# Softmax ahead of the gate's product, and turned weights split late, in a four-layer hybrid decoder

## The chip, the cores and the metric

The kernel runs on one core of one Trainium2 chip. A core has a matrix engine (TensorE; PE in the profile, PEld for its weight loads), a vector engine (VectorE, DVE), a scalar engine (ScalarE, ACT), a general engine (GpSimd, POOL) and an engine that only issues transfers (SyncE, SP). The metric is the device time of one execution in microseconds (us), taken as the median of several runs.

## The reference

Four layers with a model width of 2048 work on 256 tokens. Each layer normalises its input, makes one combined input projection, runs one of three causal mixers and four heads of attention to a memory of 256 tokens, multiplies all head outputs by SiLU of a gate, projects them back and adds them to the residual. Mixers by layer: latent attention (0), sparse attention with a top-k indexer (1), sliding window with sinks (2), latent again (0).

```python
for i in range(DEPTH):
    h = rmsnorm(x, norm_in[i])
    # kind i % 3: (queries, keys, values ..., mq, gate) = split(h @ w_in)
    self_out = mixer(...)                       # softmax(q k^T * scale + bias, masked) v per head
    mem_out = softmax(mq mk^T / 16) mv          # 4 heads of 256; mk, mv = split(mem_n @ w_mem_kv[i])
    y = concat([self_out, mem_out]) * silu(gate)    # gate has 2048 + 1024 columns
    x = x + y @ w_out[i]
return rmsnorm(x, final_norm)
```

All inputs are 32-bit floats.

## The kernel before, in words

A product of 32-bit precision is made of three products of rounded parts: each operand is split into a high part (a copy on ACT to the type fp32r) and a low part (a subtraction on DVE), and high x high, high x low and low x high are added up in PSUM. `split` does that: `copy_act` at L61, `tensor_sub` at L65. Weights come by transfers that SP issues (`stage`, L208 and L212, tile `wr`, five buffers) and are split as they come (`parts_of`: `wh`, `wl`, three buffers each).

Two routines make the projections, 16 steps of 128 rows (12 or 4 in the latent mixer). `rows_by` gives token rows: in each step it makes six products of 512 columns, L235 to L237, for two halves of tokens. `columns_by` gives columns: in each step and for two halves `j` it makes one product of 512 columns (both parts of the activations against `wh`, L254) and one of 256 (the high part against `wl`, L256), in the order L254, L256, L254, L256. Accumulators (tag "acc") have four PSUM banks; `total` (L262, L263) adds the two halves of a `columns_by` accumulator into `z`.

Every layer is worked in six parts, in the order 4, 0, 1, 2, 3, 5: parts 0 to 3 are groups of mixer heads (four heads in the latent mixer, class `Latent`; eight in the two others, class `Grouped`), parts 4 and 5 are two memory heads each (`memory_project`, `memory_attend`). A part makes its queries, keys and values, and its gate columns (`gate`: `columns_by` twice, then `z`, `hz`, a tanh `th`, and `gT`), all in `project`. Then `attend` makes the scores (`sp`, or `msp`), softmax on DVE and ACT (`masked_softmax`: tiles `u` and `e`), and turns the normalised weights.

`turned` brings two heads' softmax weights (or one memory head's) from rows of queries to rows of keys: DVE transposes blocks of 32 x 32 into `T`; POOL issues one transfer to memory (`turn<-T`, L418) and four back (`pL<-turn`, L423); ACT copies the high part `pH` (L61) and DVE makes the low part in place (`pL`, L427). `T`, `pL` and `pH` have two buffers each. The products with the values (L521, L663, L817, into `o` or `mo`) use `pH` and `pL`, and are multiplied by `gT` (`gated` or `paired`, tile `yt`) and split into `y`.

`attend` is a generator: it yields once after the turn, and then the loop over parts runs the output projection `w_out` of the part before (four chunks of 512 columns, each with 4 steps of `rows_by` and an addition to `x`, L899) ahead of this part's products:

```python
next(steps)
if pending is not None:
    w_out(*pending, False)
*_, y = steps
pending = (part, y)
```

The order of instructions on each engine is not the written one: a planner takes the program and its own estimates of times, and lets each engine take the instruction that is written first among those that it holds ready. Within an engine's queue the order is then fixed. Small tiles share buffers by tag: `u`, `e`, `bs` and the gate's `th` share tag "e" (four), `z`, `hz` and others tag "z" (three), `yt`, `hl` and others tag "t512" (three). `tc.keep_in_program_order` pins an instruction behind the one that is written before it on its engine.

## Time and profile before

| | us |
|---|---|
| median of 3 runs (lowest to highest) | 2668.21 (2661.11 to 2670.98) |
| the profiled execution | 2658.11 |
| span of its instructions | 2656.3 |
| PE busy | 2592.4 (98%) |
| PEld busy | 2224.3 (84%) |
| DVE busy | 1953.0 (74%) |
| ACT busy | 1613.6 (61%) |
| POOL busy | 267.8 (10%) |
| mean granted TensorE clock | 0.995 of full |

A busy time is the part of the span in which the engine had an instruction of the program at work. Matmuls overlap each other, and their ends are modelled, so that a busy PE may still wait for a little in between. Idle time is put down to the instruction that ended it. The stages stand in the span in this order: the memory's keys and values to about 395 us, then the four layers to about 970, 1518, 2014 and 2656 us.

### The profile page before, as it was taken

The numbers are of one execution on the slowest core, as the hardware profiler recorded it, in microseconds if no ns is written. First come the engines' busy times: TensorE is split into PE (matmuls) and PEld (weight loads), VectorE is DVE, ScalarE is ACT, GpSimd is POOL, SyncE is SP. The second block draws the span as 40 slices with busy tenths as digits, with TensorE's granted clock in tenths as the row PEclk, the third lists the DMA queues.
The fourth block names the chain that finished last, engine by engine and source line by source line (L and its number), as shares of the span: only waits on it lengthen the run. The fifth ranks groups of instructions, "written<-read, shape, count | busy, mean of one in ns | idle before, by whom it ended". The sixth has DMA issues, their size and how long they took to land. (4 is left out here: it accounts for less than half of the span.)

```text
span 2656.3 us, 42960 instructions
## 1 busy us (share of the span) xinstructions
PE 2592.4 (98%) x14143; PEld 2224.3 (84%) x14143; DVE 1953.0 (74%) x4413; ACT 1613.6 (61%) x3414; POOL 267.8 (10%) x422
## 2 busy tenths in 40 slices
PE   8999999999999999999999999999999999999997
PEld 7788888888888878888878788878788888888885
DVE  7566656677777776887779676877777767787767
ACT  6455556556665566666667465666665655666554
POOL 1000000010000110011221101211111000000011
PEclk9999999999999999999999999999999999999998
DMA  7888887577768765567787756766776667776774
GB/s 266 276 261 272 274 263 207 157 205 185 192 175 234 214 205 168 164 205 214 227 232 217 212 190 187 235 198 202 219 208 179 200 165 195 195 195 176 228 204 134
DMA packets 472563, 553.65 MB, mean 208 GB/s; under 512 B 74484, under 2 KB 357876, under 8 KB 471188
## 3 DMA queue, kind: packets, MB, share of 16 engines
q1 hardware_dynamic: 440004, 446.69, 57.2%
q0 software_dynamic: 31040, 102.33, 13.4%
q8 instruction: 111, 1.82, 0.3%
q10 hardware_dynamic: 1296, 1.90, 0.2%
q14 instruction: 112, 0.92, 0.1%
HBM read 508.77 MB, written 54.62 MB: 212 GB/s over the span
## 5 line engine op out<-in xcount | busy, mean ns | idle before, releaser
L61 ACT ACTIVATE wh<-wr 128x512 fp32r<-128x512 f32 (+2 forms) x1768 | 1068.6, 608 | 758.7 <-PE acc_g L254 184.3
L65 DVE TENSOR_TENSOR wl<-wr,wh 128x512 fp32r<-128x512 f32 (+2 forms) x1768 | 1156.2, 662 | 499.6 <-ACT wh L61 484.8
L254 PE MATMUL acc_g<-xT,wh 128*128 128x512 f32 x1536 | 520.6, 398 | 3.0 <-DVE z L263 2.9
L256 PE MATMUL acc_g<-xT,wl 128*128 128x256 f32 x1536 | 374.5, 282 | 0.0
L256 PEld LDWEIGHTS acc_g<-xT,wl 128*128 128x128 f32 x1536 | 286.7, 189 | 27.1 <-DVE wl L65 1.2
L254 PEld LDWEIGHTS acc_g<-xT,wh 128*128 128x128 f32 x1536 | 266.1, 189 | 42.7 <-DVE z L263 4.5
L236 PE MATMUL acc_wo<-wl,y 128*128 128x512 f32 x752 | 295.2, 393 | 0.0
L237 PE MATMUL acc_wo<-wh,y 128*128 128x512 f32 x752 | 294.0, 393 | 0.0
L235 PE MATMUL acc_wo<-wh,y 128*128 128x512 f32 x752 | 236.7, 396 | 8.1 <-ACT y L61 6.0
L423 POOL DMA_DIRECT2D pL<-turn x256 | 160.3, 633 | 269.2 <-DMA turn<-T 106.0
L418 POOL DMA_DIRECT2D turn<-T x64 | 48.9, 765 | 1334.5 <-DVE mn L443 455.0
L254 PE MATMUL acc_mq<-xT,wh 128*128 128x512 f32 x512 | 172.6, 397 | 1.0 <-ACT wh L61 1.0
L254 PE MATMUL acc_mk<-mT,wh 128*128 128x512 f32 x512 | 171.6, 397 | 0.0
L235 PEld LDWEIGHTS acc_wo<-wh,y 128*128 128x128 f32 x752 | 136.3, 190 | 37.6 <-ACT y L61 8.9
L237 PEld LDWEIGHTS acc_wo<-wh,y 128*128 128x128 f32 x752 | 141.9, 189 | 29.6 <-DVE y L65 1.1
L236 PEld LDWEIGHTS acc_wo<-wl,y 128*128 128x128 f32 x752 | 142.2, 189 | 29.1 <-DVE wl L65 0.7
L254 PE MATMUL acc_qn<-cT,wh 128*128 128x512 f32 x384 | 128.6, 397 | 0.0
L254 PE MATMUL acc_cq<-xT,wh 128*128 128x512 f32 x384 | 127.8, 395 | 0.0
L899 DVE TENSOR_TENSOR x<-x,acc_wo 128x512 f32<-128x512 f32 x184 | 120.9, 678 | 6.8 <-PE acc_wo L237 6.8
L427 DVE TENSOR_TENSOR pL<-pL,pH 128x768 fp32r<-128x768 f32 (+1 forms) x64 | 57.0, 891 | 92.9 <-ACT pH L61 92.8
L256 PE MATMUL acc_mq<-xT,wl 128*128 128x256 f32 x512 | 125.1, 283 | 0.0
L256 PE MATMUL acc_mk<-mT,wl 128*128 128x256 f32 x512 | 123.0, 281 | 0.0
(297 smaller groups left out, 4790.9 us busy)
## 6 DMA issues: line engine op xcount, KB each, us to landing
wr<-in_w_out_dram SPq DMA_DIRECT2D x192, 512.0 KB, 3.6
wr<-in_w_in_a_dram SPq DMA_DIRECT2D x176, 512.0 KB, 3.8
wr<-in_w_mem_kv_dram SPq DMA_DIRECT2D x128, 512.0 KB, 4.8
wr<-in_w_in_b_dram SPq DMA_DIRECT2D x112, 512.0 KB, 4.1
wr<-in_w_in_c_dram SPq DMA_DIRECT2D x104, 512.0 KB, 3.8
wr<-in_w_uq_dram SPq DMA_DIRECT2D x288, 128.0 KB, 3.4
turn<-T POOLq DMA_DIRECT2D x48, 384.0 KB, 3.9
pL<-turn POOLq DMA_DIRECT2D x192, 96.0 KB, 4.4
```

What stands on the lines that cost most here:

```text
L61: nc.scalar.activation(o, i, AF.Copy, scale=scale)
L65: nc.vector.tensor_sub(lo, src, f32(hi))
L235: nc.tensor.matmul(acc[t][:, :n], xh, wh[:, :n], start=first, stop=False)
L236: nc.tensor.matmul(acc[t][:, :n], xh, wl[:, :n], start=False, stop=False)
L237: nc.tensor.matmul(acc[t][:, :n], xl, wh[:, :n], start=False, stop=last)
L254: nc.tensor.matmul(acc[j], wh[:, o:o + P], q[:, :, kt % 4, :], start=first, stop=False)
L256: nc.tensor.matmul(acc[j][:, 0, :], wl[:, o:o + P], q[:, 0, kt % 4, :], start=False, stop=last)
L418: nc.gpsimd.dma_start(d.rearrange("m p w -> p m w"), T.rearrange("p m j n b -> p m (j n b)"))
L423: nc.gpsimd.dma_start(f32(pL)[j * 32:(j + 1) * 32, :].rearrange("p (i r) -> p i r", r=r), bass.AP(tensor=d.tensor, offset=d.offset + j * r ...
L427: nc.vector.tensor_sub(pL, f32(pL), f32(pH))
L899: nc.vector.tensor_add(xs, xs, acc[t])
```

## The change

Three things are changed. First, a part's gate columns are no longer made in `project`; `project` hands out a function, and the loop calls it after softmax and turn of the part. Second, `turned` becomes a class `Turn` in three steps: `add` transposes a head into `T`, `send` issues the five transfers, and `parts` makes `pH` and `pL`. `parts` is called right ahead of the products, and its copy on ACT is pinned behind what is written before it on ACT. The unsplit weights wait in `pL` with three buffers instead of two or, in every second pair of a `Grouped` part, in one of two spare places beside `vz`; `pH` takes its buffers from tag "T", which has three. Three chunks of the output projection of the part before run ahead of the first half of the products, and the fourth between the halves. Third, `columns_by` makes both products of 512 columns first, and then both of 256.

```diff
@@ columns_by
+                    at = [slice(k * S + j * P, k * S + (j + 1) * P) for j in range(2)]
                     for j in range(2):
-                        o = k * S + j * P
-                        nc.tensor.matmul(acc[j], wh[:, o:o + P], q[:, :, kt % 4, :],
-                                         start=first, stop=False)
-                        nc.tensor.matmul(acc[j][:, 0, :], wl[:, o:o + P], q[:, 0, kt % 4, :],
+                        nc.tensor.matmul(acc[j], wh[:, at[j]], q[:, :, kt % 4, :], start=first, stop=False)
+                    for j in range(2):
+                        nc.tensor.matmul(acc[j][:, 0, :], wl[:, at[j]], q[:, 0, kt % 4, :],
                                          start=False, stop=last)
@@ turned
-    def turned(heads, planes):
...
+    class Turn:
+        def __init__(self, n, planes, raw=None):
...
+            self.T = wk.tile([P, 768], F32, name="T", tag="T", bufs=3)[:, :self.size].rearrange(
+                "p (m j n b) -> p m j n b", m=m, j=4, n=n)
+        def add(self, s, es):
...
+                nc.vector.transpose(self.T[:, at[0]:at[-1] + 1:step, :, s, :], ...)
+        def send(self):
...
+            d = dr.tile([m, P, w], F32, name="turn", tag=f"turn{m * w}", bufs=6)
+            nc.gpsimd.dma_start(d.rearrange("m p w -> p m w"), self.T.rearrange("p m j n b -> p m (j n b)"))
+            if self.raw is None:
+                self.raw = wk.tile([P, 768], F32R, name="pL", tag="pL", bufs=3)
+            self.raw = self.raw[:, :self.size]
+            for j in range(4):
+                nc.gpsimd.dma_start(...)
+            return self
+        def parts(self):
+            pH = wk.tile([P, 768], F32R, name="pH", tag="T", bufs=3)[:, :self.size]
+            tc.keep_in_program_order(copy_act(pH, f32(self.raw)))
+            nc.vector.tensor_sub(self.raw, f32(self.raw), f32(pH))
+            return pH, self.raw
@@ memory_project (Latent.project and Grouped.project alike)
-        return nm, kT, v, qT, gate(nm, w, g0 + 2048 + part * 512)
+        return (nm, kT, v, qT), lambda: gate(nm, w, g0 + 2048 + part * 512)
@@ memory_attend (Latent.attend alike)
-            ws.append(turned([es], [(0, 0), (0, 1), (1, 0), (1, 1)]))
-        yield
+            turn.add(0, es)
+            ws.append(turn.send())
+        gT = yield
...
-            pH, pL = ws[h]
+            pH, pL = ws[h].parts()
@@ Grouped.first
+            room = [act.tile([P, 2048], F32R, name="vz", tag=f"big{1 + z}") for z in range(2)]
+            self.vz = [r[:, :1152].rearrange("p (t c) -> p t c", t=2) for r in room]
+            self.raw = [r[:, 1152:1920] for r in room]
@@ Grouped.attend
+                if n_ % 2 == 0:
+                    ws.append(Turn(2, CAUSAL, self.raw[n_ // 4] if n_ % 4 == 2 else None))
+                ws[-1].add(n_ % 2, masked_softmax(score, bias, None, nsk))
+                if n_ % 2 == 1:
+                    ws[-1].send()
+            gT = yield
...
                 for u in range(2):
+                    pp = ws[2 * z + u].parts()
@@ the loop over parts
             next(steps)
+            gT = gating()
             if pending is not None:
-                w_out(*pending, False)
-            *_, y = steps
+                w_out(*pending, False, range(3))
+            y = steps.send(gT)
+            if pending is not None:
+                w_out(*pending, False, range(3, 4))
+            y = next(steps)
             pending = (part, y)
```

## The prediction, made before the changed kernel ran

> **What bounds the kernel now.** I read the page first (busy times, then the idle time before each group), then the list of waits, then the instruction timeline and the chain of waits at the places that the waits name.

> ```profile
> span 2656.3 us, 42960 instructions
> ...
> PE 2592.4 (98%) x14143; PEld 2224.3 (84%) x14143; DVE 1953.0 (74%) x4413; ACT 1613.6 (61%) x3414; POOL 267.8 (10%) x422
> ```

> PE (TensorE) is the bound: it idles for 2656.3 - 2592.4 = 63.9 us. A change can win there, or by making the same matmuls follow each other more closely. The list of waits for PE says what ends its idle time (us in total, times, longest):

> ```profile
> PE o L817 <- ACT pH L61: 9.5, 9, 2.3
> PE mo L521 <- ACT pH L61: 8.8, 7, 2.3
> ...
> PE acc_wo L235 <- ACT y L61: 6.0, 4, 4.4
> ...
> PE acc_g L254 <- DVE z L263: 2.9, 5, 0.6
> ...
> PE o L663 <- ACT pH L61: 2.3, 5, 1.0
> ...
> PE o L817 <- DVE pL L427: 1.4, 3, 0.5
> PE mo L521 <- DVE pL L427: 1.0, 3, 0.3
> ```

> So 9.5 + 8.8 + 2.3 + 1.4 + 1.0 = 23.0 us go to the products of the turned softmax weights (`o`, `mo`), which wait for the high part `pH` or the low part `pL`. Those are late because their transfer is late, and while they wait, ACT and DVE stand still with all that is queued behind (list of waits, whole kernel):

> ```profile
> ACT pH L61 <- DMA pL<-turn: 104.3, 51, 4.7
> DVE pL L427 <- ACT pH L61: 92.8, 54, 4.9
> ```

> One such place, in a sliding-window part, in the timelines of PE and of ACT (start, duration, idle time before in brackets):

> ```profile
> 1791.64 0.28 PE L256 MATMUL acc_g<-xT,wl 128*128 128x256 f32 x1
> 1794.26 0.56 PE L817 MATMUL o<-pH,vz 128*128 128x512 f32 x1 [2.34 <-ACT pH L61]
> ```
> ```profile
> 1789.23 0.78 ACT L61 ACTIVATE e<-e,rc 128x128 f32<-128x128 f32 x2
> 1793.36 0.84 ACT L61 ACTIVATE pH<-pL 128x768 fp32r<-128x768 f32 x1 [3.35 <-DMA pL<-turn]
> ```

> ACT sits in front of `pH` for 3.35 us; the weight splits behind it cannot run, so PE runs dry. The dearest case is the end of the last layer, in the chain of waits:

> ```profile
> 2600.98 0.23 PE acc_wo L237
> ...
> 2603.94 5.68 DMA pL<-turn
> ...
> 2609.64 0.64 ACT pH L61
> ...
> 2611.62 5.40 DMA wr<-in_w_out_dram
> ...
> 2618.19 0.53 ACT y L61
> ...
> 2621.69 0.43 PE acc_wo L235
> ```

> A late `pL` holds `pH`, that holds DVE, DVE's late split frees its `wr` buffer late, the next weight load starts late, and `y` comes 4.4 us late. After that gap a 512-column matmul takes 0.43 us instead of 0.23 for about 13 matmuls (2618.76 to 2624.19): 5.43 - 13 x 0.23 = 2.4 us more.

> **Part 1: softmax, turn and transfer ahead of the gate; the split when the products come.** The same instructions run (64 turned tiles, each one `turn<-T` and four `pL<-turn` transfers, one `pH` copy, one `pL` subtraction); only their place changes. Today a transfer's cover is `w_out` of the part before: 4 chunks x 24 products x 0.23 = 22 us, from which softmax itself is taken. In the new order it is the gate (128 matmuls, 32 groups of four at 0.70 us, see part 3: 22.4 us) and three chunks (16.5 us). The way of the last turned tile in the window above:

> ```profile
> 1790.05 0.63 DVE L415 STREAM_TRANSPOSE T<-e 128x128 f32<-128x128 f32 x2
> ```
> ```profile
> 1791.09 0.75 POOL L418 DMA_DIRECT2D turn<-T  x1 [2.38 <-DVE T L415]
> 1798.99 2.48 POOL L423 DMA_DIRECT2D pL<-turn  x4 [7.15 <-PE acc_g L256]
> ```

> From T to the last issue at 1801.5 is 11.4 us, about 15 with the landing. Eight heads of a sliding part take 46 us (rows below), 6 a head; so a latent (MLA) part's four take some 23 us, a memory part's two 12, and with 15 behind them the cover of 39 us holds. In the grouped parts (sparse and sliding) it is partial. Each wait costs PE more than its idle time: a 512-column matmul is counted busy for 0.40 us, but the next may start after 0.23, so 0.16 us a wait. For `mo` and L663: 8.8 + 1.0 + 2.3 + 15 x 0.16 = 14.5 us; I take 13 of it. For L817: 9.5 + 1.4 + 12 x 0.16 = 12.8 us; I take 7, since the chain from softmax to the last products stays long there. **Term: -20** (bounds 0 and -27.3). The end of the last layer: 4.4 + 0.16 + 2.4 = 7.0 us; what is late next there is the weight load, so I take **-6** (bounds 0 and -7).

> The split's own cost at its new place:

> ```profile
> L61 ACT ACTIVATE pH<-pL x64: 613/844/850, 547.3 to 2620.5; 128x768 fp32r<-128x768 f32 x48, 128x512 fp32r<-128x512 f32 x16
> L427 DVE TENSOR_TENSOR pL<-pL,pH x64: 683/958/961, 548.0 to 2621.9; 128x768 fp32r<-128x768 f32 x48, 128x512 fp32r<-128x512 f32 x16
> ```

> 0.84 + 0.96 = 1.8 us from ACT's start to the low part. It is pinned behind the last weight split of the third chunk. With three `wh` buffers ACT may run up to three steps of 6 x 0.23 = 1.36 us ahead of PE, 4.1 us; that hides it: **0**. Without this cover it is the second rival. On POOL's queue the transfers move ahead of nothing but each other, and the next part's loads stand behind them as before; SP holds weight loads alone. No load is added, and the two spare places for raw weights and a third `pL` buffer (five instead of two) take waits away.

> **What the move costs.** Two windows, the gate alone and `w_out` with softmax beside it (columns: length, then busy of PE, PEld, DVE, ACT, POOL):

> ```profile
> 751.00:773.00 22.00, 22.00 (x127) 19.19 (x126) 13.85 (x25) 11.97 (x22) 0.00 (x0) 1.00 0.60 178
> 774.00:796.00 22.00, 22.00 (x106) 18.46 (x105) 20.51 (x64) 16.25 (x40) 3.22 (x5) 1.00 0.52 146
> ```

> With softmax beside it DVE is at 20.51 of 22 us and PE still loses nothing. `w_out` alone needs DVE for 16 splits and 8 additions; both groups stand on the page (busy us, mean ns):

> ```profile
> L65 DVE TENSOR_TENSOR wl<-wr,wh 128x512 fp32r<-128x512 f32 (+2 forms) x1768 | 1156.2, 662 | 499.6 <-ACT wh L61 484.8
> ...
> L899 DVE TENSOR_TENSOR x<-x,acc_wo 128x512 f32<-128x512 f32 x184 | 120.9, 678 | 6.8 <-PE acc_wo L237 6.8
> ```

> 16 x 0.65 + 8 x 0.66 = 15.7 us (busy time through the count), so softmax is some 5 us of DVE there, and beside the gate DVE comes to 13.85 + 5 = 19 of 22 us, less than it bears today. **0**; without this slack the third rival.

> The second cost is a queue for buffers. The timelines of PE and DVE in that latent part:

> ```profile
> 744.17 0.40 PE L648 MATMUL sp<-kn,qn 128*128 128x256 f32 x2
> ```
> ```profile
> 776.64 0.28 DVE L441 TENSOR_TENSOR u<-sp,caus 128x128 f32<-128x128 f32 x1
> ...
> 777.84 0.42 DVE L383 SCALAR_TENSOR_TENSOR gT<-th,hz 128x256 f32<-128x256 f32 x1
> ```

> The scores lay ready at 745, yet their first use `u` came at 776.64, just as the last gate tile `gT` was made. `u`, `e` and the gate's `th` share four buffers (tag "e"): they are given out in program order. In the new order `th` stands behind all `e` of the part. A sliding part:

> ```profile
> 1743.66 0.28 DVE L441 TENSOR_TENSOR u<-sp,bm 128x128 f32<-128x128 f32 x1
> 1743.87 0.42 DVE L383 SCALAR_TENSOR_TENSOR gT<-th,hz 128x256 f32<-128x256 f32 x1
> ```

> Softmax lasts from 1743.66 to 1790.05, 46 us, twice the gate. So for about 24 us the gate's last accumulator keeps one of the four PSUM banks, and `w_out` works with three. At a chunk's border the second half's bank then waits for the addition (0.68 us, row above). The first half's last product starts 0.45 before the last one, takes 0.40, the addition 0.68: its bank is free 0.63 us after the last product's start, and the next chunk wants it after 0.45. That is 0.2 us if DVE is free, 0.85 if one split is ahead. Eight grouped parts x 3 borders: 5 to 20 us, or 0 if scores fill the gap. I take **+6**, near the lower row since PE's order can take the free half first. The waits for `z` (2.9 us) come from the same shortage; I leave them: **0** (bounds -3.7 and +4).

> **Part 3: the 512-column products first.** In `columns_by` the order becomes L254 L254 L256 L256 instead of L254 L256 L254 L256. The trace already has both, since the planner moved every other step:

> ```profile
> 150.00 0.62 PE L254 MATMUL acc_mk<-mT,wh 128*128 128x512 f32 x2
> ...
> 150.70 0.40 PE L254 MATMUL acc_mk<-mT,wh 128*128 128x512 f32 x1
> ...
> 151.41 0.62 PE L254 MATMUL acc_mk<-mT,wh 128*128 128x512 f32 x2
> ...
> 152.10 0.40 PE L254 MATMUL acc_mk<-mT,wh 128*128 128x512 f32 x1
> ...
> 152.82 0.62 PE L254 MATMUL acc_mk<-mT,wh 128*128 128x512 f32 x2
> ```

> A group that starts with x2 takes 0.70 and 0.69 us (150.00, 151.41), an alternating one 0.71 and 0.72 (150.70, 152.10): 0.02 less, between 0.015 and 0.018 with rounding allowed for. The loops hold 1728 groups (gate 768, mk 256, mq 256, cq 192, qn 192, kn 64), of which half alternate: 864 x 0.018 = 15.6 us. Where PE is held by something else the gain is lost, so I take **-11** (bounds 0 and -15.6).

> [...]

> **Sum:** -20 - 6 - 11 + 6 = -31 us. The profiled execution took 2658.11 us (span 2656.3 and 1.8 around it): 2627. The median of the runs, 2668.21, lies 10.1 above it, so against the median the forecast is 2637 us.

> **Rivals.** [...]
> Second, no change: the wait moves from the transfer to the split. If ACT is not ahead of PE, each of 64 splits keeps PE for 0.4 of its 1.8 us, 26 us: 2637 + 26 = 2663. For it: ACT and DVE are at 75 to 93% in these windows. Against: three weight buffers of lead.
> Third, slower: the queue for "e" buffers. In the grouped parts gate tiles come only after 46 us of softmax, the first products' `yt` waits for them, the next part's `hl` (same buffers as `yt`, tag "t512") waits for `yt`, and softmax of the next part for `hl`. PE's other work in a part is about 74 us (q, gate, `w_out` at 22 each, products and scores 8); if the chain of softmax 46, transfer 15, split and products 5, `hl` and transposes 5 and 9 more for late gate tiles grows to 80, each of 8 parts loses 6 us: 2637 + 48 = 2685. It decides from (31 + 13) / 8 = 5.5 us a part. For it: 46 + 15 already outlasts gate and three chunks. Against: q of the next part (22 us) fills the gap.

> **How the numbers follow.** A difference under 0.5% (13 us) can hardly be told from none here. Chances: my forecast 0.55, first rival 0.20, second 0.13, third 0.12. Faster by over 0.5% (below 2655) is the first two, 0.75; within it 0.13; slower 0.12. The best case takes all bounds: 27.3 + 7 + 15.6 + 3.7 = 53.6, 2615. The range goes from 2610 (the runs spread by some us) to 2664, with the second rival and without the third. The likeliest case's own range is 2615 to 2652.

> **What would show it.** Right: the waits of `o` and `mo` for `pH` under 8 us in total; `pH` waiting for its transfer under 20 us; no gap of 4 us before the last output product; alternating groups gone; PE's idle time about 43 us. Wrong: new waits of acc_wo L235 for `x` L899, or of `o` and `mo` for `pL` in most parts; a longer way from one grouped part's first `u` to the next's; a DVE or ACT busy over 95% beside the gate.

## The result, and the profile after

The changed kernel takes 2594.78 us (median of 4 runs, 2592.04 to 2599.47) against 2667.94 for the kernel before (four runs; the three before the forecast gave 2668.21): ratio 0.9731, 95% interval 0.9707 to 0.9755. It is faster by 73 us, where 31 were forecast; the direction was right, the size was not, and the time lies below the range. The profiled execution took 2595.72 us. Three executions of later groups (one of the kernel before, one each of two variants) were slower by far, at 2795 to 10669 us, and are left out of every median and ratio below. The page of the changed kernel:

```profile
span 2593.9 us, 42976 instructions
...
PE 2559.6 (99%) x14143; PEld 2211.9 (85%) x14143; DVE 1958.3 (75%) x4413; ACT 1602.2 (62%) x3414; POOL 267.8 (10%) x422
```

The same 14143 matmuls run. PE's idle time fell from 63.9 to 34.3 us, and its busy time, which holds matmuls that run slowly or wait a little, by 32.8 us. What ends PE's idle time now (us in total, times, longest; L836, L533 are L817, L521 of before):

```profile
PE o L836 <- ACT pH L61: 6.0, 7, 2.2
PE acc_kvb L235 <- ACT wh L61: 2.9, 2, 2.1
...
PE acc_wo L235 <- ACT y L61: 1.5, 1, 1.5
...
PE mo L533 <- ACT pH L61: 0.3, 1, 0.3
```

The waits for `pH` fell from 20.6 to 6.3 us, and those for `pL` are gone; so is the 4.4 us gap ahead of the last output products (1.5 left) and every wait for `z`. ACT stands in front of `pH` for 34.9 us instead of 104.3 (list of waits, whole kernel; `vz` is here the spare place beside `vz`):

```profile
ACT pH L61 <- DMA vz<-turn: 20.6, 8, 3.9
...
ACT pH L61 <- DMA pL<-turn: 14.3, 8, 3.3
```

The groups of `columns_by` start every 0.70 us, and the alternating ones of 0.71 to 0.72 are gone (timeline of PE, the same place as before):

```profile
149.94 0.63 PE L254 MATMUL acc_mk<-mT,wh 128*128 128x512 f32 x2
...
150.64 0.62 PE L254 MATMUL acc_mk<-mT,wh 128*128 128x512 f32 x2
...
151.34 0.63 PE L254 MATMUL acc_mk<-mT,wh 128*128 128x512 f32 x2
...
152.04 0.62 PE L254 MATMUL acc_mk<-mT,wh 128*128 128x512 f32 x2
```

One thing the forecast saw in a single place only: stretches in which TensorE runs at half its clock. In the kernel before, 1795 to 1798 us, right behind the 2.34 us wait shown in the prediction, PE starts 10 matmuls, and a little later in as long a window, with about the same mix of 512 and 256 columns, 19 (length, busy of PE, PEld, DVE, ACT, POOL, then the granted clock):

```profile
1795.00:1798.00 3.00, 3.00 (x10) 2.61 (x11) 2.00 (x4) 0.77 (x2) 0.00 (x0) 0.51 0.72 259
1799.00:1802.00 3.00, 3.00 (x19) 2.63 (x18) 1.39 (x2) 1.46 (x3) 2.47 (x4) 1.00 0.86 255
```

The profile before has four such stretches while PE works (at 132, 1518, 1795 and 2617 us, 20.5 us in all); the profile after has none. PE counts as busy in them, so they hide in busy time.

To see where the 62.4 us between the two spans went, take every distance from one matmul's start to the next and subtract 0.443 ns for each column of the first (227 ns for 512 columns, near the least steady distance in these traces). What is left over sums to 164.7 us before and 101.5 after; the difference, 63.2, is that of the spans but for 0.8 us:

| over the columns' time, us | before | after | change | forecast |
|---|---|---|---|---|
| waits for `pH` and `pL` at the products | 28.0 | 7.5 | -20.5 | -20 |
| waits for `y` (the last layer's end) | 6.6 | 1.7 | -4.9 | -6, with the clock there |
| under 30 ns a matmul (the order of products) | 56.5 | 47.2 | -9.3 | -11 |
| waits for `z`, and shortage of PSUM banks | 3.7 | 0 | -3.7 | +6 |
| waits for `wh`, `wl` | 16.4 | 9.5 | -6.9 | 0 |
| matmuls at half clock | 8.5 | 0 | -8.5 | in the end's term |
| 100 to 300 ns, too short to show as idle | 21.2 | 11.8 | -9.4 | 0 |
| 30 to 100 ns | 23.8 | 23.8 | 0 | 0 |

### The profile page after: what moved, and what is told of

Read it like the earlier page. It is cut to its first block, busy times and chain, and to the rows that moved or that the text cites. A ratio compares the mean times of both kernels' runs of the same rounds, so it can differ in the third digit from the quotient of the medians.

```text
span 2593.9 us, 42976 instructions
## 1 busy us (share of the span) xinstructions
PE 2559.6 (99%) x14143; PEld 2211.9 (85%) x14143; DVE 1958.3 (75%) x4413; ACT 1602.2 (62%) x3414; POOL 267.8 (10%) x422
## 3 DMA queue, kind: packets, MB, share of 16 engines
q0 software_dynamic: 31040, 102.33, 14.2%
## 4 chain that ended last, share of the span: by engine, by line
PE 91%; DMA 4%; issue 2%; DVE 2%; POOL 1%; ACT 1%; ACTq 0%; POOLq 0%; DVEq 0%
PE acc_g L254 14%; PE acc_g L256 7%; PE acc_wo L236 6%; PE acc_wo L235 6%; PE acc_wo L237 6%; PE acc_mk L254 5%; PE acc_mq L254 4%; PE acc_qn L254 3%; PE acc_cq L254 3%; PE acc_mk L256 2%; PE acc_mq L256 2%; PE acc_mv L236 2%; PE acc_mv L237 2%; PE acc_mv L235 2%; PE acc_qn L256 2%; PE acc_cq L256 2%
## 5 line engine op out<-in xcount | busy, mean ns | idle before, releaser
L61 ACT ACTIVATE wh<-wr 128x512 fp32r<-128x512 f32 (+2 forms) x1768 | 1071.7, 609 | 841.7 <-PE acc_g L254 141.4
L65 DVE TENSOR_TENSOR wl<-wr,wh 128x512 fp32r<-128x512 f32 (+2 forms) x1768 | 1164.9, 663 | 526.4 <-ACT wh L61 495.0
L254 PE MATMUL acc_g<-xT,wh 128*128 128x512 f32 x1536 | 485.7, 396 | 0.0
L256 PEld LDWEIGHTS acc_g<-xT,wl 128*128 128x128 f32 x1536 | 283.8, 188 | 61.8
L256 PE MATMUL acc_g<-xT,wl 128*128 128x256 f32 x1536 | 304.9, 279 | 0.0
L237 PE MATMUL acc_wo<-wh,y 128*128 128x512 f32 x752 | 292.9, 390 | 0.0
L235 PE MATMUL acc_wo<-wh,y 128*128 128x512 f32 x752 | 239.5, 391 | 1.5 <-ACT y L61 1.5
L254 PEld LDWEIGHTS acc_g<-xT,wh 128*128 128x128 f32 x1536 | 235.8, 189 | 0.7
L237 PEld LDWEIGHTS acc_wo<-wh,y 128*128 128x128 f32 x752 | 141.3, 188 | 27.2
L235 PEld LDWEIGHTS acc_wo<-wh,y 128*128 128x128 f32 x752 | 138.5, 188 | 29.4 <-ACT y L61 1.9
L254 PE MATMUL acc_mk<-mT,wh 128*128 128x512 f32 x512 | 160.8, 396 | 2.0 <-ACT wh L61 2.0
L254 PE MATMUL acc_mq<-xT,wh 128*128 128x512 f32 x512 | 162.1, 396 | 0.0
L429 POOL DMA_DIRECT2D pL<-turn x192 | 120.8, 636 | 208.5 <-DMA turn<-T 139.3
L254 PE MATMUL acc_qn<-cT,wh 128*128 128x512 f32 x384 | 121.5, 398 | 0.0
L254 PE MATMUL acc_cq<-xT,wh 128*128 128x512 f32 x384 | 120.8, 396 | 0.0
L918 DVE TENSOR_TENSOR x<-x,acc_wo 128x512 f32<-128x512 f32 x184 | 119.9, 679 | 0.7
L256 PEld LDWEIGHTS acc_mk<-mT,wl 128*128 128x128 f32 x512 | 95.8, 188 | 22.7 <-DVE wl L65 0.4
L256 PEld LDWEIGHTS acc_mq<-xT,wl 128*128 128x128 f32 x512 | 93.5, 188 | 20.5 <-DVE wl L65 1.4
L256 PE MATMUL acc_mq<-xT,wl 128*128 128x256 f32 x512 | 102.7, 280 | 0.6 <-DVE wl L65 0.6
```

The lines of the kernel that those rows point to most:

```text
L61: return nc.scalar.activation(o, i, AF.Copy, scale=scale)
L65: nc.vector.tensor_sub(lo, src, f32(hi))
L235: nc.tensor.matmul(acc[t][:, :n], xh, wh[:, :n], start=first, stop=False)
L237: nc.tensor.matmul(acc[t][:, :n], xl, wh[:, :n], start=False, stop=last)
L254: nc.tensor.matmul(acc[j], wh[:, at[j]], q[:, :, kt % 4, :], start=first, stop=False)
L256: nc.tensor.matmul(acc[j][:, 0, :], wl[:, at[j]], q[:, 0, kt % 4, :], start=False, stop=last)
```

## The experiments

Each kernel was timed beside the kernel before on one chip; ratios are to it. Chips differ between groups (by group, the median of the kernel before lay between 2667.94 and 2677.55 us), so kernels are compared by ratio, or directly within a group.

**One part at a time.** First the order of products alone, put into the kernel before.

```diff
                     for j in range(2):
-                        matmul(acc[j], wh ...); matmul(acc[j][:, 0, :], wl ...)
+                        matmul(acc[j], wh ...)
+                    for j in range(2):
+                        matmul(acc[j][:, 0, :], wl ...)
```

> The kernel before with part 3 alone (both 512-column products of columns_by first). Theory A, the order itself is worth 10 to 18 ns in each of the 864 groups that alternated: 9 to 16 us, so 2652 to 2659 against 2668; PE's idle time stays near 64 us and the waits for pH stay at 20 us or more; the clock stays near 0.995. Rival 1, the order is worth nothing: 2668 within 4. Rival 2, the order carries most of the 73 us (each group also has its low part later, so that waits for wl go): below 2640.

Measured: 2689.57 us, ratio 1.0057 (1.0041 to 1.0072): slower by 15 us, which no theory had. The order did what it should: the row "under 30 ns" fell from 56.5 to 46.9 us. But the waits grew (list of waits for PE; `L817`, `L521` and `L663` are the products with `pH`):

```profile
PE o L817 <- ACT pH L61: 16.3, 12, 4.5
PE acc_wo L235 <- ACT y L61: 12.2, 4, 7.3
PE mo L521 <- ACT pH L61: 12.2, 7, 2.8
PE acc_g L254 <- DVE z L263: 7.7, 5, 1.5
...
PE o L663 <- ACT pH L61: 6.3, 5, 2.6
```

34.8 us for `pH` where it was 20.6, 12.2 for `y` where it was 6.0, 7.7 for `z` where it was 2.9; matmuls at half clock took 22.7 us more than their columns' time instead of 8.5. While a transfer sets when the products may start, a faster PE arrives sooner and waits longer; that alone would take the gain away but make no loss. The longer half-clock time (14.2 us more) can make it one, and so can the planner, which made a new order for the whole program: the instructions on ACT stand in another order at 1457 of 3414 places, those on DVE at 2302 of 4413. The run does not separate the two. In the changed kernel the old order was put back:

```diff
-                    for j in range(2): matmul(acc[j], wh ...)
-                    for j in range(2): matmul(acc[j][:, 0, :], wl ...)
+                    for j in range(2): matmul(acc[j], wh ...); matmul(acc[j][:, 0, :], wl ...)
```

> The changed kernel with the old order of the products (512, 256, 512, 256) put back. Theory A: 9 to 16 us slower than the changed kernel, 2604 to 2611, half of the groups alternating, waits of PE as in the changed kernel. Rival 1: 2595 within 4. Rival 2: above 2625.

Measured: 2611.97 us, ratio 0.9766 (0.9753 to 0.9779), against 0.9731 with the new order (0.9714 when it was timed again, below): 9 to 14 us more. "Under 30 ns" is 56.2 us again, 9.0 above the changed kernel, and waits and clock add a few us. So the new order gains here, and was a loss without the rest.

Then the gate behind softmax, with `w_out` in three chunks and one, but the turn and the early split as before (the order of products kept):

```diff
-            return ..., gate(self.nm, self.w, self.g0 + g * 512)
+            return (...), lambda: gate(self.nm, self.w, self.g0 + g * 512)
...
+            gT = gating()      # after next(steps); turned() unchanged
```

> The order of part 3 and the gate behind softmax, with w_out in 3 + 1 chunks, but the old turn: the split stands right behind the transfers in the program, two buffers each for T, pL and pH. Theory A, half of the gain of the move comes from ACT and DVE no longer standing in front of pH: ACT still idles 50 us or more in front of pH, and the time is 2615 to 2645. Rival, cover is all that counts (the transfers land early, so the place of the split is idle talk): ACT's idle time in front of pH falls below 35 us as in the changed kernel, and the time is 2595 to 2605.

Measured: 2642.46 us, 0.9878 (0.9862 to 0.9894), in theory A's range. And the late split, but the gate at its old place (in the memory parts alike):

```diff
                 at, gating = mixer.project(part)
+                gT = gating()
                 steps = mixer.attend(*at)
             next(steps)
-            gT = gating()
```

> The order of part 3 and the late, pinned split with five places and 3 + 1 chunks, but the gate at its old place ahead of softmax. Theory A: ACT's idle time in front of pH falls below 45 us and memory and latent parts lose their waits; 2605 to 2630. Rival, cover is all that counts: with only w_out's 16 us of three chunks between softmax and the products PE waits more than before for pH, over 25 us, and the time is 2640 or more.

Measured: 2671.23 us, 0.9983 (0.9968 to 0.9998). The time is that of its rival (cover), and ACT's idle time too stays above what theory A had. Lists of waits, first of the gate moved alone, then of the split moved alone:

```profile
ACT pH L61 <- DMA pL<-turn: 108.5, 46, 4.4
...
PE acc_wo L235 <- ACT wh L61: 10.1, 6, 2.0
```
```profile
ACT pH L61 <- DMA pL<-turn: 77.2, 31, 5.8
...
PE mo L533 <- ACT pH L61: 15.9, 6, 3.2
```

In the second run ACT waits another 20.8 us for transfers into the spare places. With the early split ACT still stands in front of `pH` for 108.5 us, and PE now also waits 10.1 us for `wh`, the splits that queue behind it. With the late split and without the cover, `mo` alone waits 15.9 us. Measured from the order alone (1.0057), the gate's move brings 1.8% of the time before, the late split 0.7%, both together 3.3%, more than their sum.

**The transfers taken away.** To see whether all this is the transfers' doing, the kernel before (with the new order, nothing else moved) splits straight from `T`. This leaves out the exchange of the 32 x 32 blocks and the bytes of these transfers:

```diff
-        nc.gpsimd.dma_start(d..., T...)          # and the four back into pL
-        copy_act(pH, f32(pL)); nc.vector.tensor_sub(pL, f32(pL), f32(pH))
+        copy_act(pH, T); nc.vector.tensor_sub(pL, T, f32(pH))
```

> The kernel before with part 3 and without the five transfers of each turn: pH and pL are split straight from T, so the blocks of 32 are left unexchanged (that part of the computation is left out). Gate, softmax and w_out stay at their old places. Theory A, what the moves won is the wait for these transfers and what hangs on it (blocked splits, the slow clock after long gaps), and the order of part 3 earns its 10 us once the waits are gone: 2580 to 2605, no slow-clock stretch between the layers, waits for pH under 8 us. Rival, the old place of the gate costs time by itself (softmax late, DVE crowded beside w_out): over 2620.

Measured: 2586.04 us, 0.9682 (0.9655 to 0.9709), as theory A had it. PE's list of waits has no `pH`, `y` or `z` left (it begins with):

```profile
PE gp L92 <- DMA rows<-in_mem_norm_dram: 7.0, 1, 7.0
PE acc_qr L236 <- DVE wl L65: 3.5, 8, 0.5
PE acc_kvb L235 <- ACT wh L61: 1.8, 1, 1.8
```

No stretch at half clock fell between the layers (mean granted clock 0.998). The bytes taken off memory are hardly the reason: weight loads of 512 KB land in 3.6 to 5.2 us (medians) against 3.6 to 4.8 in the kernel before. So no cost of the gate's old place shows once the transfers are gone; the kernel before paid for the transfers, by 3.2% with the order.

**What each detail of the late split does.** The same group held three variants of the changed kernel.

```diff
-            tc.keep_in_program_order(copy_act(pH, f32(self.raw)))
+            copy_act(pH, f32(self.raw))
```

> The changed kernel without the pin on the copy of pH. Theory A, the planner then puts the copy early, where it holds the transfer as landed, and ACT stands in front of it as before: ACT idles over 60 us in front of pH; 2615 to 2645, near the kernel with the gate moved alone (2642). Rival, the place in the written order is enough: ACT's idle time stays near 35 us, and the time within 5 us of 2595.

Measured: 2607.74 us, 0.9758 (0.9732 to 0.9784), below theory A's range. ACT's wait in front of `pH`, 14.3 us with the pin for the ordinary places, is

```profile
ACT pH L61 <- DMA pL<-turn: 61.4, 31, 4.3
```

and 20.9 more for the spare places. ACT stands there again as theory A had it, but the time follows only in part: by ratios the version without the pin lies 7 us above the changed kernel (12 against the 0.9714 of its second timing), with intervals that overlap. The written order does most of the work.

```diff
-                self.raw = wk.tile([P, 768], F32R, name="pL", tag="pL", bufs=3)
+                self.raw = wk.tile([P, 768], F32R, name="pL", tag="pL", bufs=2)
-                    ws.append(Turn(2, CAUSAL, self.raw[n_ // 4] if n_ % 4 == 2 else None))
+                    ws.append(Turn(2, CAUSAL, None))
```

> The changed kernel with two places for unsplit weights (two buffers of pL, no spare place beside vz) instead of five. Theory A: in the grouped parts the third and fourth turned tile must wait for the first products, so that their transfers lie open: waits for pH of L836 grow by 1 to 3 us in each of 8 parts, 2605 to 2630; latent and memory parts are unchanged. Rival, the softmax of eight heads is the longer chain and the places do not matter: within 5 us of 2595.

Measured: 2605.55 us, 0.9747 (0.9723 to 0.9771), in theory A's range at its lower end, though by ratio only 4 to 9 us above the changed kernel. The list of waits:

```profile
PE o L836 <- ACT pH L61: 12.8, 8, 3.3
```

That is 6.8 us more than with five places, in the grouped parts as expected, and the trace has two stretches at half clock.

```diff
-                w_out(*pending, False, range(3))
+                w_out(*pending, False)
             y = steps.send(gT)
-            if pending is not None: w_out(*pending, False, range(3, 4))
```

> The changed kernel with all four chunks of w_out ahead of the products, none between their halves. Theory A, the first half is covered 5.5 us longer, the second loses 5.5 us of cover and its split stands right behind the first half's: within 6 us of 2595, more waits for pL. Rival, the chunk between the halves carries the second half's split: 2605 or more.

Measured: 2596.22 us, 0.9719 (0.9696 to 0.9742). The total hardly moves, as theory A had it; the waits do:

```profile
PE acc_wo L235 <- ACT y L61: 7.7, 5, 1.9
...
PE o L836 <- ACT pH L61: 0.4, 2, 0.3
```

The fourth chunk ahead of the products covers the grouped parts' last transfers (6.0 to 0.4 us), but at the four layer ends `y` lies open for 1.7 to 1.9 us each, since the next `w_out` needs it at once.

**The step that had been priced at 6 us.** The buffers of tag "e" are indeed given out in written order, as the prediction read it. In a sliding part of the changed kernel the gate's columns were done at 1706.9 us, yet its first tile comes 23 us later, near the end of softmax (timelines of PE and DVE):

```profile
1706.48 0.39 PE L256 MATMUL acc_g<-xT,wl 128*128 128x256 f32 x2
```
```profile
1729.52 0.42 DVE L383 SCALAR_TENSOR_TENSOR gT<-th,hz 128x256 f32<-128x256 f32 x1
...
1738.40 0.63 DVE L418 STREAM_TRANSPOSE T<-e 128x128 f32<-128x128 f32 x2
```

To see what that costs, `th` got a buffer of its own, and in a second kernel the shared buffers became five:

```diff
-                th = wk.tile([P, S], F32, name="th", tag="e", bufs=4)
+                th = wk.tile([P, S], F32, name="th", tag="th", bufs=1)
```
```diff
-    tag="e", bufs=4        # u, e, bs, th
+    tag="e", bufs=5
```

> The changed kernel with one buffer of its own for the gate's th, so that the gate no longer waits for the last of softmax's tiles and its accumulators are given back at once. Theory A, the accumulator held for some 24 us in the eight grouped parts costs PE nothing, since the planner finds other products: within 5 us of 2595. Rival, the step of the prediction that priced it at 6 us (bounds 0 and 20): 2575 to 2590.

> The changed kernel with five buffers for u, e, bs and th instead of four. Theory A, softmax of eight heads (49 us) is what the last grouped products still wait for, and it is held by these buffers: softmax gets some us shorter, the waits of L836 for pH (6 us idle) fall below 3: 2588 to 2594. Rival, softmax is held by its place in the queues of ACT and DVE: within 3 us of 2595.

Measured: 2601.03 us, 0.9719 (0.9691 to 0.9747), and 2598.86 us, 0.9713 (0.9687 to 0.9740). Neither gains; theory A for the five buffers missed. With `th` on its own the wait that the forecast feared is gone, and the list shows

```profile
PE o L836 <- ACT pH L61: 11.3, 9, 2.5
```

That is 5.3 us more than in the changed kernel; that gate tiles made early get in softmax's way is a guess. PE's waits for `wh` and `wl` and the distances of 100 to 300 ns fell by some 7 us together, so giving the accumulator back early may help a little there; the total gains nothing. Five buffers do not shorten the waits either (7.2 us for L836).

**A better version.** All four chunks ahead of the products, except in a layer's last part:

```diff
-                w_out(*pending, False, range(3))
+                w_out(*pending, False, range(3 if part == 5 else 4))
             y = steps.send(gT)
-            if pending is not None:
+            if pending is not None and part == 5:
                 w_out(*pending, False, range(3, 4))
```

> The changed kernel with all four chunks of w_out ahead of the products, except in the last part of a layer, where the fourth chunk stays between the halves. Theory A, with the whole w_out ahead the waits of L836 for pH go (7.5 to about 1.5 us), and the chunk between the halves is needed only where w_out of the same part follows at once (four layer ends at 1.9 us in the kernel with the whole w_out ahead): 2587 to 2592. Rival, the slow clock and other waits take it back: 2594 to 2600.

Measured: 2585.63 us, 0.9664 (0.9637 to 0.9691). With five buffers of "e" besides:

> The same as the kernel with the whole w_out ahead except in the last part, and five buffers for u, e, bs and th. Theory A: 2585 to 2592, as near as a kernel with the transfers may come to the one without them (2586). Rival: no better than the one with four buffers, within 3 us of it.

Measured: 2597.85 us, 0.9708 (0.9681 to 0.9735), 12 us above the version with four buffers, which neither theory had; the waits of L836 are back at 6.8 us. Why a fifth buffer does that was not found. The better version was then run beside the changed kernel on one chip:

> The changed kernel once more, beside the next one on the same chip. Theory A: 2593 to 2600, its ratio to the kernel before within 0.970 to 0.976.

> The kernel with the whole w_out ahead except in the last part, once more, beside the changed kernel. Theory A: 6 to 11 us below it. Rival, the difference was one of chips: within 3 us of it.

Measured: 2596.50 us, 0.9714 (0.9693 to 0.9736), and 2585.54 us, 0.9677 (0.9656 to 0.9698): 11 us below it, with no overlap (2592.28 to 2598.19 and 2583.77 to 2588.53). L836's row in the two lists, the changed kernel first:

```profile
PE o L836 <- ACT pH L61: 6.9, 7, 2.0
```
```profile
PE o L836 <- ACT pH L61: 0.6, 2, 0.4
```

It stands level with the kernel without transfers (0.9682).

**The slow clock by itself.** Into the better version a pause of PE was put at the start of layers 1, 2 and 3, with one or two small transfers in it:

```diff
+            tc.keep_in_program_order(matmul(held[:, :8], ident, ident[:, :8]))
+            nc.vector.tensor_copy(hop[0], held[:, :8]); nc.gpsimd.dma_start(hop[1], hop[0])
+            back = tc.keep_in_program_order(matmul(held[:, 8:16], ident, hop[1]))
+            with tc.issue_after(back.ins):
                 mixer.first()
```

> The kernel with the whole w_out ahead except in the last part, and with a pause of PE put in at the start of layers 1, 2 and 3: a tiny product, a copy, one transfer from buffer to buffer, and a tiny product that waits for it, with the layer's first products behind. It measures the slow clock by itself. Theory A, a pause of about 3 us is followed by a stretch of 3.4 us or more at half the clock, so each costs its length and 1.5 to 3.5 us more: 12 to 20 us over the same kernel without pauses. Rival, a pause costs its length alone: 6 to 11 us, no slow stretch in the records.

> The same with two transfers in a row in each of the three pauses, about 5 us each. Theory A: 18 to 28 us over the kernel without pauses, a slow stretch of 3.4 or 6.8 us behind each. Rival: 13 to 17 us, no slow stretch.

Measured: 2625.87 us, 0.9826 (0.9805 to 0.9847), and 2633.32 us, 0.9854 (0.9832 to 0.9876), that is 40.3 and 47.8 over the version without pauses on the same chip. Both are more than either theory had, because the pinned product also laid open the layer's normalisation, so that each pause came to some 10 us and not 3. PE's list of waits with one transfer, and two windows behind the first pause:

```profile
PE spr L179 <- DVE dg L178: 17.2, 3, 5.8
...
PE held L918 <- DMA hop<-hop: 7.1, 3, 2.4
PE tp L187 <- DVE x L930: 3.1, 6, 0.7
```
```profile
987.60:991.60 4.00, 4.00 (x11) 3.13 (x12) 0.43 (x1) 0.63 (x1) 0.54 (x2) 0.50 1.07 317
993.00:997.00 4.00, 4.00 (x19) 3.29 (x18) 2.08 (x3) 1.79 (x4) 0.00 (x0) 1.00 0.67 207
```

By starts of matmuls the pauses themselves take some 30 of the 42.3 us between the spans. Matmuls at half clock behind them, 11 in 4 us instead of 19, take 11.1 us, some 3.7 a pause; another 1.7 us fell into a stretch at 394 us, which no pause caused. The kind is theory A's, the numbers are not. The second transfer adds some 6 us to the pauses and hardly anything to the slow stretches (11.6 us).

## Why the prediction was right or wrong

The move was right in kind, and its three main terms came near their size. What failed is the rest of the sum. Of the 42 us by which the forecast was short, 9.7 come from the shortage of PSUM banks and the waits for `z` (+6 forecast, -3.7 measured), 16.3 from what hangs on a blocked ACT (nothing forecast), about 6 from the slow clock ahead of the last layer's end (nothing forecast), and 11 from the offset of 10.1 us between profile and median, which did not carry over. Two of the forecast's own signs missed the same way: `pH` waits 34.9 us for its transfers and not under 20, and PE's idle time is 34.3 us and not 43.

- **Waits of the products, -20:** -20.5 in the trace. That grouped parts would keep some of theirs was right too (6.0 us at L836).
- **End of the last layer, -6:** right in mechanism and size, -4.9 and 2.5 of the clock.
- **Order of products, -11:** its direct effect was -9.3: 0.70 against 0.71 to 0.72 us a group, and 9.0 us of spacing back with the old order in the changed kernel. But the forecast added the term to the others as if it stood alone. Put into the kernel before alone, with all that the planner then moved, it was +15.
- **Shortage of PSUM banks, +6:** the step that failed in sign. Its queue is there, its price is not: no wait for `x` L918 stands in PE's list, `z` fell from 2.9 us to nothing, and freeing the bank brought no net gain. That PE had enough other products is the likely reason, not a shown one.
- **Split at its new place, 0:** right in that PE waits for `pL` nowhere over 0.2 us, but the pin behind it was not priced (7 to 12 us by ratios, not clear of the scatter). A slip there, 6 x 0.23 as 1.36 and not 1.38 us, changes nothing.
- **What hangs on a blocked ACT, 0:** the first term that was missing. The prediction says itself that the weight splits behind a blocked `pH` cannot run and that PE runs dry by it, and it shows the two rows of 104.3 and 92.8 us; yet only waits by the names `pH` and `pL` were summed. The waits for `wh` and `wl` (-6.9) and those too short to show as idle (-9.4) went as well; without the transfers they are as low (8.6 and 11.3 us are left in that trace), as they would be if they hung on them.
- **The slow clock:** the second. It was priced at one place; the trace had it at four (-8.5 in all), and it varies from run to run: over 45 runs of the kernel before, three at a granted clock of 0.995 average 2667.8 us and three at 0.990 average 2680.4; the changed kernel runs at 0.997 to 0.999. The 10.1 us by which the median lay above the profiled execution were no constant to be carried over: the changed kernel's median lies 0.9 us below its profiled execution. That they were mostly clock is likely, not shown, since the clock of those three runs is not on record and the profiled execution's own was 0.995.

Of the rivals, none came: in the complete change the order gained (0.9731 against 0.9766 with the old one), the wait did not move to the split, and the queue for "e" slowed nothing that the total shows.

## What to carry to other kernels

When an engine stands in front of a late transfer, price everything that is queued behind it, not only the wait that bears its name, and put the work that needs the transfer where it is used, pinned, with places enough for all that is under way. A gain on the bounding engine may count only once the waits ahead of it are gone, and taken alone it may even lose (here the order gained 9 to 14 us with the rest, and the run with it alone was 15 us slower), so run the parts apart before adding their terms. Look at the granted clock before taking a profile's waits as the whole cost.

## What was not expected of the hardware

TensorE dropped to half its clock (0.50 to 0.51 in the windows) behind pauses that were not long: the stretch at 1795 us followed 2.34 us of idle. Stretches last 3.4 us or a multiple (3.413 and 6.827 us in the clock records of the kernel before, 10.2 with the order alone, 13.7 with the pauses).
